# Two more raw tiles in the ring that loads the first FFN's weights and the conditioning matrix

## The chip, the cores and the metric

The kernel runs on one core of one Trainium2 chip. The metric is the device time of one execution in microseconds. The core has five engines with an instruction stream each: PE (matrix products), DVE (element-wise work), ACT (casts and activations), POOL, and SP, which here issues nearly all DMAs. Each works through its own stream in order and waits on semaphores of the others.

## The reference, cut to what matters

One layer of a diffusion backbone: 512 latent tokens and 256 context tokens of width 1024. The first part is what the change touches. All shifts, scales and gates come from one matrix product of a vector with `w_ada` (1024 x 9216), and the first FFN (width 2816, SwiGLU) runs on both token sets:

```python
mod_x = (silu(c) @ w_ada + b_ada).reshape(bsz, 9, 1, d)
mod_c = (silu(c_ctx) @ w_ada + b_ada).reshape(9, 1, d)

def ffn_sublayer(h, m, i, w_up, w_down):
    shift, scale, gate = sub_mod(m, i)
    a, b = split(modulate(h, shift, scale) @ w_up, 2)
    y = (silu(a) * b) @ w_down
    return post_ln(ALPHA * h + 0.5 * gate * y, ln_g[i], ln_b[i])

x = ffn_sublayer(x, mod_x, 0, ffn1_w_in, ffn1_w_out)
ctx = ffn_sublayer(ctx, mod_c, 0, ffn1_w_in, ffn1_w_out)
```

Neighbourhood attention, a gated delta rule and a second FFN follow; the change doesn't edit them.

## The kernel before

Every weight matrix comes from HBM in tiles of 128 x 1024 float32 (512 KB). A tile is loaded by SP into a raw tile `wr`, cast by ACT to `wh` (line 135) and split by DVE into the remainder `wl = wr - wh` (line 137); three matmuls (`wh` with the high and the low part of the activations, `wl` with the high part) then make one product of nearly full precision. A tile of the conditioning matrix (`w_adaT`) is also loaded into a `wr`, but is read by DVE alone: line 279 multiplies it with the vector and sums along the row (its result tile is `adap`), once for the latent tokens, or twice where the context needs the section too.

In the first FFN all raw tiles come from one function, `raw1` (line 320), in turn: two buffers of the pool `w` and one of the pool `w1x`, so a ring of three. SP issues a load when the reader of the load three places earlier is done. The loads of `Stream.fill` (line 172, up and down weights; two weight tiles make one unit f of the FFN's width, a and b of the SwiGLU), of `modulate_k` (line 351), of `ada_gen` (line 300) and of the tokens (lines 435, 474) share it. The first three units' weights are an exception: `start_f` (line 400) loads them into tiles `ac`.

The stages, with their place in the profiled span:

- 0 to 61.5 us: for each of eight slices k of the width, two matrix tiles give the latent shift and scale (`modulate_k`), PE transposes the normalised tokens (line 358), ACT modulates and splits them into `uxh` and `uxl`, and the products of units 0 to 2 with that slice are made (lines 411 to 413, accumulators `acc`).
- 61.5 to 126.5: units 3 to 7 for the latent tokens (lines 190 to 192, `ps<-uxh`), while `modulate_k` makes the context's shift and scale.
- 126.5 to 221.8: units 0 to 7 for the context (`ps<-uch`), then units 8 to 10 for both, with four matrix tiles a unit from `ada_gen` (`ada_step(4)`).
- 221.8 to 312: the down product of units 0 to 10 (line 209), latent, then context.
- 312 to 504: the second up-phase, units 11 to 21 for both token sets, each with four matrix tiles.
- from 504: the down product of units 11 to 21 and the rest of the layer.

```python
def up_phase(hx, hc, fs):
    for f in fs:
        A, B = ws.get(), ws.get()
        hx.append(h_x())
        ffn_unit(tp, pp, A, B, uxh, uxl, NX, *hx[-1])
        hc.append(h_c())
        ffn_unit(tp, pp, A, B, uch, ucl, NCT, *hc[-1])
        ada_step(4)
```

The order of instructions on each engine isn't written by hand: a scheduler in the build sets it with a timeline of its own, in which free buffers count. The pool `t1` (`tp`, line 343) holds the temporaries of the first FFN (`fs`, `adap`, `crow`) and is closed at line 484.

Of the kernel before, what the change touches and what calls it, by code (L numbers as in the profile page):

```python
# [18 lines left out]
P = 128  # L19
D = 1024  # L20
# [38 lines left out]
def body(ctx, tc, I, out, dbg=None):  # L59
# [4 lines left out]
    def pool(name, side="left", space=None):  # L64
        kw = dict(name=name, bufs=1, reuse_waits="tile")
        if space is not None:
            kw["space"] = space
        else:
            kw["side"] = side
        g = tc.tile_pool(**kw)  # L70
        st = ExitStack()
        p = st.enter_context(g)
        return p, st.close
# [3 lines left out]
    def tl(p, shape, tag, bufs=1, dt=F32):  # L77
        uid[0] += 1
        return p.tile(list(shape), dt, name=f"{tag}_{uid[0]}", tag=tag, bufs=bufs)
# [214 lines left out]
    def ada_gen(tp, wp, crow):  # L294
        for sec in range(2, 9):
            which = [(0, colx)] + ([(1, colc)] if sec < 5 else [])
            sl = slice(sec * 8, sec * 8 + 8)
            for k in range(KT):
                raw = raw1()
                nc.sync.dma_start(raw[:], I["w_adaT"][sec * KT + k])  # L300
                for w, col in which:
                    dot_cols(tp, raw, crow[:, w], col, sec * 8 + k)
                if k < KT - 1:
                    yield
            for w, col in which:
                V.scalar_tensor_tensor(col[:, sl], col[:, sl], float(sec % 3 == 1), bcol[:, sl], op0=ALU.add, op1=ALU.add)
                if (w, sec) in gates:
                    to_row(tp, pp, col[:, sl], gates[(w, sec)])
            yield
# [5 lines left out]
    wp, close_wp = pool("w")  # L315
    WB = 2
    wx, close_wx = pool("w1x")
    raws = [0]

    def raw1():  # L320
        raws[0] += 1
        return tl(wx, [P, D], "wr") if raws[0] % 3 == 0 else tl(wp, [P, D], "wr", WB)

    ap_, close_ap = pool("acc1")
    hcp, close_hcp = pool("hc1")
# [15 lines left out]

    hxp, close_hxp = pool("hx1", "right")
    tp, close_tp = pool("t1")
    xn = {"x": [], "c": []}

    def modulate_k(pp, kind, k):

        w, col, uh, ul, n = (0, colx, uxh, uxl, NX) if kind == "x" else (1, colc, uch, ucl, NCT)
        for sec in range(2):
            raw = raw1()  # L350
            nc.sync.dma_start(raw[:], I["w_adaT"][sec * KT + k])
            dot_cols(tp, raw, crow[:, w], col, sec * 8 + k)
        for sec in range(2):
            c0 = sec * 8 + k
            V.scalar_tensor_tensor(col[:, c0:c0 + 1], col[:, c0:c0 + 1], float(sec), bcol[:, c0:c0 + 1], op0=ALU.add, op1=ALU.add)
        ps = tl(pp, [P, n], "ps", PSB[0])
        for t, x_t in enumerate(xn[kind]):
            T.transpose(ps[:, t * P:(t + 1) * P], x_t[:, k * P:(k + 1) * P], ident)
        u32 = tl(tp, [P, NX], "fs", 2)
        S.activation(u32[:, 0:n], ps[:], AF.Identity, bias=col[:, k:k + 1], scale=col[:, 8 + k:9 + k])  # L360
        split(u32[:, 0:n], uh[:, k], ul[:, k])
# [71 lines left out]
    for t in range(2):  # L433
        raw = raw1()
        nc.sync.dma_start(raw[:], tok_src("c", t))
        xn["c"].append(tl(ap_, [P, D], f"ac{t}"))
        ln_norm(tp, xn["c"][t][:], raw, act=True)
# [43 lines left out]
    hx, hc = up_phase([], [], range(HF, NF))  # L481
    for _ in ada:
        pass
    close_tp()
    close_up()

# [953 lines left out]
    tp, close_tp = pool("t2")  # L1440
# [247 lines left out]
```

## Time and profile before

| what | us |
|---|---|
| median of 3 runs (lowest, highest) | 1540.94 (1540.72, 1541.74) |
| time of the profiled execution | 1542.48 |
| its span | 1540.7 |

| stretch of the span, us | PE busy | DVE busy | DMA share | GB/s |
|---|---|---|---|---|
| 0 to 61.5 | 47.33 | 44.95 | 0.79 | 271 |
| 61.5 to 126.5 | 60.76 | 41.42 | 0.66 | 209 |
| 126.5 to 221.8 | 95.30 | 65.47 | 0.59 | 187 |
| 221.8 to 316 | 93.92 | 41.79 | 0.47 | 151 |
| 316 to 504 | 181.72 | 115.17 | 0.59 | 188 |
| 504 to 1540 | 986.67 | 740.07 | 0.40 | 129 |

Rows of the profile name an engine, a line of the kernel, the operation, the tiles as out<-in and, in brackets, how long the engine stood idle before it and what ended that. Matmuls are pipelined and their ends are modelled, so a PE without idle time isn't always at its full pace; the number of matmuls in a stretch tells more. SPq is the queue of SP: how its DMA issues follow each other.

### The profile page before, as it was taken

The numbers are of one execution on the slowest core, as the hardware profiler recorded it, in microseconds if no ns is written. First come the engines' busy times: TensorE is split into PE (matmuls) and PEld (weight loads), VectorE is DVE, ScalarE is ACT, GpSimd is POOL, SyncE is SP. The second block draws the span as 40 slices with busy tenths as digits, with TensorE's granted clock in tenths as the row PEclk, the third lists the DMA queues.
The fourth block names the chain that finished last, engine by engine and source line by source line (L and its number), as shares of the span: only waits on it lengthen the run. The fifth ranks groups of instructions, "written<-read, shape, count | busy, mean of one in ns | idle before, by whom it ended". The sixth has DMA issues, their size and how long they took to land.

```text
span 1540.7 us, 23656 instructions
## 1 busy us (share of the span) xinstructions
PE 1465.7 (95%) x9221; PEld 1257.3 (82%) x9221; DVE 1048.9 (68%) x1792; ACT 604.2 (39%) x1005; POOL 228.7 (15%) x224
## 2 busy tenths in 40 slices
PE   6999999999999999999997799999999999999997
PEld 4779988888788888898976687867778999998886
DVE  8566672577555487577758887566578699887426
ACT  5435321212211335645633443366525455344310
POOL 0000000000000021132300101167532023220001
PEclk9999999999999999999999899999999999999999
DMA  9666563556555623332377544173353233324422
GB/s 320 201 200 207 180 193 101 187 178 205 181 181 178 200 106 125 99 101 90 99 203 202 153 130 132 64 254 120 110 191 117 89 110 124 110 97 151 137 83 82
DMA packets 107586, 230.72 MB, mean 150 GB/s; under 512 B 34177, under 2 KB 47825, under 8 KB 107473
## 3 DMA queue, kind: packets, MB, share of 16 engines
q1 hardware_dynamic: 105312, 221.79, 45.2%
q10 hardware_dynamic: 1586, 5.32, 0.9%
q0 software_dynamic: 576, 2.10, 0.4%
q8 instruction: 72, 1.18, 0.3%
q14 instruction: 40, 0.33, 0.1%
HBM read 206.33 MB, written 22.85 MB: 149 GB/s over the span
## 4 chain that ended last, share of the span: by engine, by line
PE 62%; DMA 14%; DVE 13%; issue 5%; ACT 3%; POOL 2%; SPq 1%; DVEq 0%; ACTq 0%; POOLq 0%
PE ps L209 18%; DMA wr<-in_w_adaT_dram 8%; PE pm L190 5%; PE pm L192 5%; PE pm L191 5%; PE ps L192 4%; PE ps L190 4%; PE ps L191 4%; PE ps L1475 3%; PE ps L1476 3%; PE ps L1477 3%; DVE wl L137 3%; PE pc L854 3%; DVE adap L279 2%; DMA wr<-in_up_dram 1%
## 5 line engine op out<-in xcount | busy, mean ns | idle before, releaser
L137 DVE TENSOR_TENSOR wl<-wr,wh 128x1024 fp32r<-128x1024 f32 (+1 forms) x215 | 265.4, 1240 | 169.9 <-ACT wh L135 169.6
L135 ACT CAST wh<-wr 128x1024 fp32r<-128x1024 f32 (+1 forms) x215 | 217.5, 1017 | 340.5 <-PE ps L209 76.2
L279 DVE SCALAR_TENSOR_TENSOR adap<-wr,crow 128x1024 f32<-128x1024 f32 x112 | 137.0, 1223 | 93.8 <-DMA wr<-in_w_adaT_dram 92.3
L192 PE MATMUL ps<-uxh,wl 128*128 128x512 f32 (+1 forms) x496 | 181.5, 367 | 5.7 <-DVE wl L137 5.7
L190 PE MATMUL ps<-uxh,wh 128*128 128x512 f32 (+1 forms) x496 | 181.5, 369 | 4.8 <-ACT wh L135 4.7
L191 PE MATMUL ps<-uxl,wh 128*128 128x512 f32 (+1 forms) x496 | 180.6, 365 | 0.2 <-DVE uxl L137 0.2
L112 POOL TENSOR_TENSOR rs<-ve,mhalf 128x1 f32<-128x1 f32 (+2 forms) x46 | 49.9, 1088 | 762.3 <-DVE ve L108 752.6
L190 PE MATMUL pm<-uxh,wh 128*128 128x512 f32 x320 | 133.0, 416 | 4.3 <-ACT spill L606 2.3
L192 PE MATMUL pm<-uxh,wl 128*128 128x512 f32 x320 | 128.4, 401 | 0.4 <-DVE wl L137 0.4
L191 PE MATMUL pm<-uxl,wh 128*128 128x512 f32 x320 | 127.8, 399 | 0.0
L192 PEld LDWEIGHTS ps<-uxh,wl 128*128 128x128 f32 x496 | 94.4, 190 | 24.5 <-DVE wl L137 9.9
L190 PEld LDWEIGHTS ps<-uxh,wh 128*128 128x128 f32 x496 | 94.3, 191 | 21.4 <-ACT wh L135 7.3
L191 PEld LDWEIGHTS ps<-uxl,wh 128*128 128x128 f32 x496 | 94.7, 191 | 14.4 <-DVE uxl L137 0.4
L190 PE MATMUL ps<-uch,wh 128*128 128x256 f32 x352 | 98.6, 280 | 0.0
L192 PE MATMUL ps<-uch,wl 128*128 128x256 f32 x352 | 98.3, 279 | 0.0
L191 PE MATMUL ps<-ucl,wh 128*128 128x256 f32 x352 | 98.3, 279 | 0.0
L209 PE MATMUL ps<-wh,hx 128*128 128x512 f32 x352 | 94.8, 389 | 0.0
L209 PEld LDWEIGHTS ps<-wh,hx 128*128 128x128 f32 x352 | 65.9, 188 | 13.5
L190 PEld LDWEIGHTS pm<-uxh,wh 128*128 128x128 f32 x320 | 61.8, 193 | 16.3 <-ACT spill L606 2.7
L135 ACT CAST hx<-fs 128x512 fp32r<-128x512 f32 x22 | 13.7, 620 | 154.0 <-DVE fs L272 154.0
L192 PEld LDWEIGHTS pm<-uxh,wl 128*128 128x128 f32 x320 | 61.5, 192 | 14.8 <-DVE wl L137 1.5
L191 PEld LDWEIGHTS pm<-uxl,wh 128*128 128x128 f32 x320 | 61.7, 193 | 10.7
(411 smaller groups left out, 3485.4 us busy)
## 6 DMA issues: line engine op xcount, KB each, us to landing
wr<-in_w_adaT_dram SPq DMA_DIRECT2D x88, 512.0 KB, 4.0
wr<-in_up_dram SPq DMA_DIRECT2D x80, 512.0 KB, 3.6
wr<-in_dn_dram SPq DMA_DIRECT2D x58, 512.0 KB, 3.6
wr<-in_win_dram SPq DMA_DIRECT2D x52, 512.0 KB, 3.9
rb<-in_up_dram SPq DMA_DIRECT2D x18, 512.0 KB, 3.5
wr<-in_w_o_dram SPq DMA_DIRECT2D x8, 512.0 KB, 4.1
ac<-in_up_dram SPq DMA_DIRECT2D x6, 512.0 KB, 5.0
Dt<-gcd SPq DMA_DIRECT2D x12, 256.0 KB, 5.4
```

What stands on the lines that cost most here:

```text
L112: G.tensor_tensor(rs[:], ve[:], mhalf[:, 0:n], ALU.pow)
L135: S.copy(hi, src)
L137: V.tensor_tensor(lo, src, hi.bitcast(F32), ALU.subtract)
L190: T.matmul(ps, a, uh[:, k, :], start=(k == 0), stop=False)
L191: T.matmul(ps, a, ul[:, k, :], start=False, stop=False)
L192: T.matmul(ps, b, uh[:, k, :], start=False, stop=(k == nk - 1))
L209: T.matmul(banks[t][d][:, c0:c1], a[:, sl], b[:, d * 512 + c0:d * 512 + c1], start=first and j == 0, stop=last and j == 2)
L279: V.scalar_tensor_tensor(pr[:], raw[:], 1.0, crow, op0=ALU.mult, op1=ALU.mult, accum_out=col[:, c:c + 1])
L854: last[0] = T.matmul(*a, **k).ins
L1475: T.matmul(ps[:], a, uh[:, k], start=k == 0, stop=False)
L1476: T.matmul(ps[:], a, ul[:, k], start=False, stop=False)
L1477: T.matmul(ps[:], b, uh[:, k], start=False, stop=k == 3)
```

## The change

`raw1` takes a second pool into its turn while `more[0]` is set: of five raw tiles, two come from `w`, two from `t1` and one from `w1x`. `more[0]` is set when `t1` is opened, ahead of the first stage, and cleared when the last matrix tile has been taken, just ahead of closing `t1`. The loads behind that use the ring of three again.

```diff
-    raws = [0]
+    raws, more = [0], [None]
 
     def raw1():
         raws[0] += 1
-        return tl(wx, [P, D], "wr") if raws[0] % 3 == 0 else tl(wp, [P, D], "wr", WB)
+        k = raws[0] % (5 if more[0] else 3)
+        return tl(more[0], [P, D], "wr", 2) if k > 2 else tl(wx, [P, D], "wr") if k == 0 else tl(wp, [P, D], "wr", WB)
...
     tp, close_tp = pool("t1")
+    more[0] = tp
...
     for _ in ada:
         pass
+    more[0] = None
     close_tp()
```

The scheduler's order moves with it on every engine. On SP, in the first stage, before (`wr` from `in_w_adaT` are matrix tiles, `ac` from `in_up` the weights of units 0 to 2):

```order
L351 DMA wr_207<-in_w_adaT_dram 128x1024
L351 DMA wr_211<-in_w_adaT_dram 128x1024
L351 DMA wr_258<-in_w_adaT_dram 128x1024
L400 DMA ac_61_226<-in_up_dram 128x1024
L351 DMA wr_262<-in_w_adaT_dram 128x1024
L351 DMA wr_321<-in_w_adaT_dram 128x1024
L400 DMA ac_65_233<-in_up_dram 128x1024
L351 DMA wr_325<-in_w_adaT_dram 128x1024
L400 DMA ac_75_277<-in_up_dram 128x1024
L351 DMA wr_358<-in_w_adaT_dram 128x1024
L351 DMA wr_362<-in_w_adaT_dram 128x1024
L400 DMA ac_79_284<-in_up_dram 128x1024
```

And the same place now (two lines of the file lower, so line 353 is 351 and 402 is 400):

```order
L353 DMA wr_321<-in_w_adaT_dram 128x1024
L402 DMA ac_61_226<-in_up_dram 128x1024
L353 DMA wr_325<-in_w_adaT_dram 128x1024
L353 DMA wr_358<-in_w_adaT_dram 128x1024
L402 DMA ac_65_233<-in_up_dram 128x1024
L353 DMA wr_362<-in_w_adaT_dram 128x1024
L353 DMA wr_395<-in_w_adaT_dram 128x1024
L353 DMA wr_399<-in_w_adaT_dram 128x1024
L402 DMA ac_75_277<-in_up_dram 128x1024
L353 DMA wr_432<-in_w_adaT_dram 128x1024
L353 DMA wr_436<-in_w_adaT_dram 128x1024
L402 DMA ac_79_284<-in_up_dram 128x1024
```

The last four `ac` loads stand behind two, two, four and four more matrix tiles than before.

On PE, at the end of the same stage, before (line 358 transposes the tokens for k = 7, `acc` are the accumulators of the six products):

```order
L411 MATMUL acc_290<-uxh_87,hx_286 128x512
L412 MATMUL acc_290<-uxl_88,hx_286 128x512
L413 MATMUL acc_290<-uxh_87,hx_287 128x512
L358 MATMUL ps_479<-ident_64,ax_15_104 128x128
L358 MATMUL ps_479<-ident_64,ax_16_106 128x128
L358 MATMUL ps_479<-ident_64,ax_17_108 128x128
L358 MATMUL ps_479<-ident_64,ax_18_110 128x128
L411 MATMUL acc_193<-uxh_87,wh_189 128x512
L411 MATMUL acc_200<-uxh_87,wh_196 128x512
L411 MATMUL acc_232<-uxh_87,wh_228 128x512
```

And what stands ahead of the products of the last slices now (line 413 is 411, 414 is 412, 415 is 413):

```order
L414 MATMUL acc_283<-uxl_88,hx_279 128x512
L415 MATMUL acc_283<-uxh_87,hx_280 128x512
L413 MATMUL acc_290<-uxh_87,hx_286 128x512
L414 MATMUL acc_290<-uxl_88,hx_286 128x512
L415 MATMUL acc_290<-uxh_87,hx_287 128x512
L413 MATMUL acc_193<-uxh_87,wh_189 128x512
L414 MATMUL acc_193<-uxl_88,wh_189 128x512
L415 MATMUL acc_193<-uxh_87,wl_190 128x512
L413 MATMUL acc_200<-uxh_87,wh_196 128x512
L414 MATMUL acc_200<-uxl_88,wh_196 128x512
```

The transposes `ps_479` have moved well ahead, and the 36 products of the last two slices follow each other without one between them.

On SP, in the second up-phase, before (line 300 loads matrix tiles, line 172 weight tiles; `wr_3643` and `wr_3649` are the two of one unit, `wr_3783` and `wr_3789` of the next):

```order
L172 DMA wr_3643<-in_up_dram 128x1024
L172 DMA wr_3649<-in_up_dram 128x1024
L300 DMA wr_3767<-in_w_adaT_dram 128x1024
L300 DMA wr_3779<-in_w_adaT_dram 128x1024
L300 DMA wr_3771<-in_w_adaT_dram 128x1024
L300 DMA wr_3775<-in_w_adaT_dram 128x1024
L172 DMA wr_3783<-in_up_dram 128x1024
L172 DMA wr_3789<-in_up_dram 128x1024
```

And now:

```order
L172 DMA wr_3643<-in_up_dram 128x1024
L300 DMA wr_3767<-in_w_adaT_dram 128x1024
L300 DMA wr_3638<-in_w_adaT_dram 128x1024
L300 DMA wr_3771<-in_w_adaT_dram 128x1024
L172 DMA wr_3789<-in_up_dram 128x1024
L300 DMA wr_3775<-in_w_adaT_dram 128x1024
L300 DMA wr_3907<-in_w_adaT_dram 128x1024
L172 DMA wr_3649<-in_up_dram 128x1024
L300 DMA wr_3911<-in_w_adaT_dram 128x1024
L300 DMA wr_3779<-in_w_adaT_dram 128x1024
L172 DMA wr_3783<-in_up_dram 128x1024
```

The two tiles of a unit no longer follow each other. Of those that are loaded later than before, `wr_3649` stands five rows further back in SP's whole order, `wr_3783` three and `wr_3924`, of the unit after, six; `wr_3789` stands four rows further ahead. From the down product of units 11 to 21 on, the order is the same but for a few rows that change places on each engine.

## The prediction

> **What bounds the kernel now.** I read the page's first part, then the busy time of the engines by stretch, then what PE waits for, and last the chain of waits in the stretch that loses time. On the page:
>
> ```profile
> span 1540.7 us, 23656 instructions
> PE 1465.7 (95%) x9221; PEld 1257.3 (82%) x9221; DVE 1048.9 (68%) x1792; ACT 604.2 (39%) x1005; POOL 228.7 (15%) x224
> PE ps L209 18%; DMA wr<-in_w_adaT_dram 8%; PE pm L190 5%; PE pm L192 5%; PE pm L191 5%; PE ps L192 4%; PE ps L190 4%; PE ps L191 4%; PE ps L1475 3%; PE ps L1476 3%; PE ps L1477 3%; DVE wl L137 3%; PE pc L854 3%; DVE adap L279 2%; DMA wr<-in_up_dram 1%
> ```
>
> PE is the bound as a whole, so only its losses can be won back. But 8% of the chain that ended last is loads of the conditioning matrix into `wr`, the raw tile that the change multiplies. `wr` is cast and split (ACT L135, DVE L137) or multiplied and summed (DVE L279). The next table, busy time by stretch, shows where PE pays (columns: stretch, its length, PE, PEld, DVE, ACT, POOL busy with instruction counts, granted clock, DMA share, GB/s).
>
> ```profile
> 20.00:40.00 20.00, 20.00 (x87) 15.84 (x86) 18.96 (x37) 10.89 (x14) 0.00 (x0) 1.00 0.93 308
> 61.50:126.50 65.00, 60.76 (x257) 48.51 (x257) 41.42 (x78) 23.09 (x39) 0.00 (x0) 0.95 0.66 209
> 312.40:378.75 66.35, 66.35 (x385) 58.65 (x384) 51.84 (x85) 14.12 (x21) 0.00 (x0) 1.00 0.57 183
> 395.35:504.30 108.95, 102.67 (x579) 87.23 (x577) 56.03 (x88) 23.15 (x39) 0.00 (x0) 1.00 0.56 177
> ```
>
> 312.4 to 378.75 holds four units of the second up-phase (96 matmuls each): 66.35 / 4 = 16.59 us a unit, PE without a gap. 395.35 to 504.3 holds six of the same units in 108.95 us, 18.16 each. DMA is at 0.56 and DVE at 56 of 109 us there, so neither is full. What PE waits for, in 61.5 to 126.5 (the first two rows) and in 316 to 504 (the last two); us, times, longest:
>
> ```profile
> PE ps L190 <- ACT wh L135: 2.7, 1, 2.7
> PE ps L192 <- DVE wl L137: 1.4, 2, 0.7
> ...
> PE ps L192 <- DVE wl L137: 4.3, 6, 1.6
> PE ps L190 <- ACT wh L135: 2.0, 4, 1.0
> ```
>
> PE waits for split weights. Why these are late is in DVE's timeline and in the chain of waits of the same 18 us:
>
> ```profile
> 446.19 1.23 DVE L279 SCALAR_TENSOR_TENSOR adap<-wr,crow 128x1024 f32<-128x1024 f32 x1 [1.66 <-DMA wr<-in_w_adaT_dram]
> 447.46 1.23 DVE L279 SCALAR_TENSOR_TENSOR adap<-wr,crow 128x1024 f32<-128x1024 f32 x1
> 453.16 1.23 DVE L279 SCALAR_TENSOR_TENSOR adap<-wr,crow 128x1024 f32<-128x1024 f32 x1 [4.46 <-DMA wr<-in_w_adaT_dram]
> 456.62 1.23 DVE L137 TENSOR_TENSOR wl<-wr,wh 128x1024 fp32r<-128x1024 f32 x1 [0.25 <-ACT wh L135]
> ...
> 447.46 1.24 DVE adap L279 x2
> 448.72 4.34 DMA wr<-in_w_adaT_dram
> ...
> DVE adap L279 <- DMA wr<-in_w_adaT_dram: 62.3, 25, 5.3
> ...
> 444.56 3.22 SPq L172 DMA_DIRECT2D wr<-in_up_dram  x2
> 448.72 10.95 SPq L300 DMA_DIRECT2D wr<-in_w_adaT_dram  x4
> ```
>
> This is a loop. The dot at 447.46 frees its tile; only then, at 448.72, does SP issue the next load; it lands 4.34 us later; DVE stands 4.46 us for it, and the gate product (L272) and the splits of weights that landed earlier stand behind that dot, because DVE works in order. From 317 to 505 DVE stands 62.3 us for such loads. A raw tile is held for issue, landing and reading: 3 tiles at 18.16 / 6 = 3.03 us a load (a unit takes two weight tiles and four of the matrix) are 9.1 us each. Five tiles with the same holding time would allow a load every 1.82 us, while PE at full pace asks for one every 16.59 / 6 = 2.77 us. So with five the ring is no bound there.
>
> **The change part by part, and the sum.** No arithmetic, transfer or byte goes away: the 512 KB loads and their readers are the same. Two tiles are added to the rotation, the scheduler's order moves with them, and after the second up-phase the ring has three again.
>
> *Second up-phase.* Six units at the undisturbed pace take 6 x 16.59 = 99.5 us, so 108.95 - 99.5 = 9.4 us are the loss. I take 9.4 as won; the lower bound is zero (the rivals), the upper bound is this loss itself. Next late would be DVE: 56 of 99.5 us, no bound; then the DMA engines: 177 GB/s x 108.95 / 99.5 = 194, against 308 that the same engines moved from 20 to 40 us.
>
> *Units 3 to 7 of the first up-phase (61.5 to 126.5).* Here the matmuls wait in the same way, and the clock falls once:
>
> ```profile
> 106.75 0.79 PE L190 MATMUL ps<-uxh,wh 128*128 128x512 f32 x1 [2.75 <-ACT wh L135]
> ...
> 311.96 0.39 PE L209 MATMUL ps<-wh,hc 128*128 128x512 f32 x1
> ...
> 221.91 54.23 PE ps L209 x239
> ...
> 103.40:106.80 3.40, 0.65 (x4) 0.23 (x2) 2.54 (x7) 1.04 (x1) 0.00 (x0) 1.00 0.47 141
> 106.80:110.20 3.40, 3.35 (x7) 2.25 (x8) 1.59 (x3) 1.92 (x3) 0.00 (x0) 0.50 0.87 227
> 110.20:113.60 3.40, 3.40 (x16) 2.78 (x16) 3.40 (x6) 0.62 (x1) 0.00 (x0) 1.00 0.73 243
> ```
>
> Waits: 2.7 + 1.4 = 4.1 us. Idle time is counted from a matmul's shown end, 0.39 us behind its start, while undisturbed ones start every 54.23 / 239 = 0.227 us (the rows at 311.96 and 221.91): 0.16 more for each wait, 0.5 for three. Behind the 2.75 us wait the granted clock is 0.50 for 3.4 us: 7 matmuls instead of 16, 9 x 3.4 / 16 = 1.9 us. Together 6.5 us. The Trainium skill (TensorE: Matmul & The Clock Gate, "HAM oscillation — how this bites in real kernels") puts the rule abstractly as no PE-idle gap over about 3.4 us. By that rule a gap of 2.75 us would be followed by no drop and removing it would give back no clock: the sum would be 1.9 us smaller. The trace has the drop after 2.75 us and decides. Loads rise here to 209 x 65 / 58.5 = 232 GB/s, DVE to 41.4 of 58.5 us; both fit.
>
> *Start (to 61.5).* From 20 to 40 us DVE is busy 18.96 of 20 and DMA 0.93, so more tiles buy no pace. What moves is order: PE's one wait at the end of the stage,
>
> ```profile
> 55.25 0.98 PE L411 MATMUL acc<-uxh,wh 128*128 128x512 f32 x3 [1.52 <-ACT uxh L135]
> 59.60 1.98 PE L290 MATMUL ps<-crow,one_row 1*128 1x512 f32 x4
> 62.40:65.80 3.40, 3.40 (x10) 2.65 (x9) 2.63 (x5) 2.00 (x4) 0.00 (x0) 0.50 0.89 287
> 65.80:69.20 3.40, 3.40 (x17) 2.77 (x16) 3.07 (x7) 0.82 (x2) 0.00 (x0) 0.99 0.19 39
> ```
>
> loses its reason, since the transposes for k = 7 now stand well ahead of the products that need them. I take 1.5. The clock's fall at 62.4 (10 matmuls for 17, 7 x 0.2 = 1.4 us) follows this wait and the L290 products; it can stay or go, so 0.7. The other side: four loads of the first units' weights are issued behind more of the matrix (below). The last was issued at 27.95; four places at 20 us x 308 GB/s = 11.7 loads, 1.7 us each, make it 6.8 us later:
>
> ```profile
> 27.95 0.33 SPq L400 DMA_DIRECT2D ac<-in_up_dram  x1
> DMA to landing us min/median/max: 4.0/5.0/7.8
> L137 DVE TENSOR_TENSOR hx<-ac,hx x3: 1220/1226/1227, 26.7 to 34.0; 128x1024 fp32r<-128x1024 f32 x3
> ```
>
> Issued at 34.8 it lands by 39.8 and is split by 42.2 (DVE's last such split was at 34.0, 6 us after its issue). Its 24 matmuls, 5.5 us, can be done in the 17 us to 59.6. I price it at 0, and up to +6.8 at the far end.
>
> *Context's down product (from 280 to 316).* Its only wait is 0.2 us; the ring's rows there are one load per six matmuls. I take 0.3, bounds 0 and 1.
>
> *From 504 on.* Ring and tiles are as before; a few rows swap places because the scheduler starts from other times. No resource is added. I take 0, bounds -4 and +4 (the size of the longest wait for a load shown above, 4.46 us).
>
> Sum: 9.4 + 6.5 + 1.5 + 0.7 + 0.3 = 18.4 us. The profiled execution took 1542.5 us (span 1540.7); less 18.4 is 1524.1. The median of the runs is 1540.94, 1.5 less than that execution, which gives **1522.5 us**.
>
> **Rivals.** *In part (0.15).* DVE stays in order, and in the changed rows more dots than before can stand ahead of a split. If a third to a half of the waits only move to another unit, 6 to 9 us of the 18 remain lost: 1528.5 to 1532. For it: 25 waits of DVE on this load, the longest 5.3 us, show that one late load holds everything. Against: a load that finds a free tile is issued before its turn, not after it.
>
> *No change (0.04).* The transfers themselves could be the limit, so that more of them at once only land later: 1541. For it: loads issued close together land later (4.0 to 7.8 us at the start, 3.4 to 4.8 from 400 to 500).
>
> ```profile
> DMA to landing us min/median/max: 3.4/3.9/4.8
> ```
>
> Against: 308 GB/s against the 177 in use. That the tiles aren't used at all is excluded by the rows of the order.
>
> *Slower (0.05).* In the second up-phase the order of SP now lets a unit's second weight tile be loaded behind a tile of the next unit and four of the matrix: `wr_3649` goes five places back, `wr_3783` three, `wr_3924` six. SP works in order, so if the ring keeps its pace of 3.03 us a load, these come 15, 9 and 18 us later. In hand is some 7 us (the loads issued at 444.56 and about 3 us later land in 3.4 to 4.8 and are multiplied from 456.6 on). PE then waits 8 + 2 + 11 = 21 us: 1562. It decides at the pace p: two more tiles ahead put 2p more in hand, so five and six places cost 5p - 7 - 2p and 6p - 7 - 2p, 5.4 us together at p = 2.77 (three places cost nothing), while the 36 loads of the six units win 36 x (3.03 - p), 9.4. The two are equal at p = 2.86; above it the new order loses more than the tiles win. Against it: at 3.03 a load each of five tiles would be held for 15 us, and the rows show 9.
>
> **How the numbers follow.** Forecast (0.76): 1522.5, own range 1517 to 1528 (downward 0.7 for the rest of the clock's fall, 0.7 in the down product and 4 behind 504; upward 0.7, 0.3 and 4). In part 0.15, no change 0.04, slower 0.05. The range 1517 to 1532 holds the forecast's own range, the late landing at the start (1529.3) and the case in part. A measurement of this kernel tells about 0.2% (3 us) from no change: faster 0.91 (forecast and part), same 0.04, slower 0.05.
>
> **What would show it.** Right: the last six units of the second up-phase in 99 to 101 us; PE's waits for `wl` and `wh` at L190 and L192 under 2 us in both stretches; no half clock between 100 and 125; DVE's 62.3 us for matrix loads far smaller, SP issuing them while three older ones are unread; DMA near 194 GB/s in the last six units. Wrong in the start: L411 to L413 waiting for `hx` weights between 30 and 45. Wrong in the order: PE waiting once in two units, several us at a time, for the second weight tile. If everything before 504 is 18 us earlier and the end is not, the rest lies behind.

## The result, and the profile after

The changed kernel takes 1528.59 us (median of 4 runs, 1525.19 to 1530.66), the kernel before 1541.34 us beside it (4 runs, 1540.72 to 1547.03). The ratio is 0.9904, its 95% interval 0.9887 to 0.992: faster by some 15 us. The profiled execution of the changed kernel is its slowest run, 1530.66 us. Three more series of it, shown below, have medians of 1525.76 to 1526.46; one execution in them, of 2926.64 us, stands apart from all others and is left out.

From the page of the changed kernel: its span, the first row of busy time, and the chain that ended last by line.

```profile
span 1528.8 us, 23646 instructions
PE 1462.6 (96%) x9221; PEld 1258.7 (82%) x9221; DVE 1050.0 (69%) x1792; ACT 605.4 (40%) x1005; POOL 226.8 (15%) x224
PE ps L209 19%; PE ps L190 8%; PE ps L192 8%; PE ps L191 8%; PE pm L190 5%; PE pm L192 5%; PE pm L191 5%; PE pc L857 2%; PE ps L1478 2%; PE ps L1480 2%; PE ps L1479 2%; DVE wl L137 2%; PE po L1266 1%; DMA T<-rd 1%; PE pt L1255 1%
```

Busy times are those of before, to 3 us on PE and 1 us on DVE: nothing was computed less. The matrix loads, 8% of the chain before, are no longer among the lines of the chain, and the products at L190 to L192 stand in their place.

Busy time by stretch of the changed kernel, at the places of the four rows quoted in the prediction (20 to 40 us; units 3 to 7; the first four units of the second up-phase; its last six):

```profile
20.00:40.00 20.00, 20.00 (x89) 15.63 (x89) 19.97 (x39) 10.88 (x14) 0.00 (x0) 1.00 0.98 365
59.30:118.60 59.30, 57.06 (x257) 46.47 (x257) 41.82 (x78) 23.77 (x40) 0.00 (x0) 1.00 0.69 231
303.60:369.95 66.35, 66.35 (x386) 58.76 (x385) 58.26 (x96) 15.54 (x24) 0.00 (x0) 1.00 0.71 231
386.55:486.00 99.45, 99.45 (x580) 88.00 (x578) 52.86 (x81) 23.75 (x37) 0.00 (x0) 1.00 0.50 165
```

The last six units take 99.45 us in place of 108.95 and PE has no gap; units 3 to 7 take 59.3 in place of 65, at full clock. In the first four units DMA now moves 231 GB/s in place of 183 and DVE handles 96 instructions in place of 85: the matrix is read ahead there, and the last six units have less of it left, 165 GB/s in place of 177. What is left of the waits for split weights, PE's from 59 to 119 (first row), and DVE's from 308 to 486 (the other two; before it had 62.3 us on the first of them):

```profile
PE ps L192 <- DVE wl L137: 2.2, 2, 1.9
...
DVE adap L279 <- DMA wr<-in_w_adaT_dram: 23.3, 19, 3.0
DVE fs L272 <- PE ps L192: 20.3, 12, 6.7
```

From 307 to 486 PE waits for nothing. DVE now waits for PE's products as long as for loads: the roles of the loop have turned round.

The end of the first stage in PE's timeline, where it had waited 1.52 us at 55.25:

```profile
57.05 0.39 PE L415 MATMUL acc<-uxh,hx 128*128 128x512 f32 x1
57.37 1.98 PE L290 MATMUL ps<-crow,one_row 1*128 1x512 f32 x4
59.28 0.50 PE L190 MATMUL ps<-uxh,wh 128*128 128x512 f32 x1
```

No wait, and units 3 to 7 begin at 59.3 in place of 61.5. The table sets the stages of both profiled executions side by side; each is read from the start of its first product to that of the next stage's. (Attention begins with the first `pm` product, takes in the delta rule and ends where the transposes that open the second FFN begin; these, 0.8 us, are in no row of the table.)

| stage, us | before | after | difference | predicted |
|---|---|---|---|---|
| start | 61.5 | 59.3 | -2.2 | -2.2 |
| units 3 to 7 | 65.1 | 59.3 | -5.8 | -6.5 |
| context's units, units 8 to 10, latent down product | 155.1 | 155.1 | 0 | 0 |
| context's down product | 30.8 | 29.9 | -0.9 | -0.3 |
| second up-phase | 191.9 | 182.4 | -9.5 | -9.4 |
| **to its end** | **504.3** | **486.0** | **-18.3** | **-18.4** |
| second down product and what follows it | 124.6 | 124.6 | 0 | 0 |
| attention | 533.6 | 535.9 | +2.3 | 0 |
| second FFN to the end | 377.4 | 381.5 | +4.1 | 0 |

Ahead of the second down product all that was predicted is there; 6.4 us of it are missing at the end. The rows of the last two stages, before and after (attention; the second FFN with its 0.8 us of transposes):

```profile
628.90:1162.60 533.70, 498.00 (x3668) 413.99 (x3669) 381.76 (x772) 249.74 (x474) 153.03 (x150) 0.98 0.45 138
1162.60:1540.70 378.10, 365.67 (x2423) 334.66 (x2421) 273.31 (x389) 149.37 (x225) 58.05 (x42) 0.99 0.33 111
```

```profile
610.60:1146.50 535.90, 501.15 (x3668) 415.95 (x3668) 380.85 (x770) 249.58 (x474) 153.24 (x149) 0.97 0.44 137
1146.50:1528.80 382.30, 367.52 (x2422) 335.54 (x2422) 275.11 (x389) 147.97 (x225) 55.52 (x42) 0.99 0.33 109
```

The instructions are the same to one or two. Either these stages differ from one execution to the next (in attention the granted clock is 0.97 against 0.98), or the changed order of rows costs something there. The experiments are about this, and about how many tiles the loop needs and where.

### The profile page after: what moved, and what is told of

The parts are those of the page before. It is cut to its first block, busy times and chain, and to the rows that moved or that the text cites. A ratio compares the mean times of both kernels' runs of the same rounds, so it can differ in the third digit from the quotient of the medians.

```text
span 1528.8 us, 23646 instructions
## 1 busy us (share of the span) xinstructions
PE 1462.6 (96%) x9221; PEld 1258.7 (82%) x9221; DVE 1050.0 (69%) x1792; ACT 605.4 (40%) x1005; POOL 226.8 (15%) x224
## 4 chain that ended last, share of the span: by engine, by line
PE 76%; DVE 10%; DMA 7%; issue 3%; ACT 2%; POOL 2%; SPq 0%; DVEq 0%; ACTq 0%; POOLq 0%
PE ps L209 19%; PE ps L190 8%; PE ps L192 8%; PE ps L191 8%; PE pm L190 5%; PE pm L192 5%; PE pm L191 5%; PE pc L857 2%; PE ps L1478 2%; PE ps L1480 2%; PE ps L1479 2%; DVE wl L137 2%; PE po L1266 1%; DMA T<-rd 1%; PE pt L1255 1%
## 5 line engine op out<-in xcount | busy, mean ns | idle before, releaser
L192 PE MATMUL ps<-uxh,wl 128*128 128x512 f32 (+1 forms) x496 | 179.6, 363 | 2.2 <-DVE wl L137 2.2
L190 PE MATMUL ps<-uxh,wh 128*128 128x512 f32 (+1 forms) x496 | 179.6, 365 | 0.0
L190 PE MATMUL pm<-uxh,wh 128*128 128x512 f32 x320 | 133.0, 416 | 4.1 <-ACT spill L609 2.1
L192 PE MATMUL pm<-uxh,wl 128*128 128x512 f32 x320 | 128.2, 401 | 0.7 <-DVE wl L137 0.7
L192 PEld LDWEIGHTS ps<-uxh,wl 128*128 128x128 f32 x496 | 93.7, 189 | 17.9 <-DVE wl L137 3.3
L190 PEld LDWEIGHTS ps<-uxh,wh 128*128 128x128 f32 x496 | 93.4, 189 | 14.3 <-issue 0.8
L190 PE MATMUL ps<-uch,wh 128*128 128x256 f32 x352 | 98.6, 280 | 0.0
L192 PE MATMUL ps<-uch,wl 128*128 128x256 f32 x352 | 98.3, 279 | 0.0
L190 PEld LDWEIGHTS pm<-uxh,wh 128*128 128x128 f32 x320 | 61.6, 193 | 16.3 <-ACT spill L609 3.0
L192 PEld LDWEIGHTS pm<-uxh,wl 128*128 128x128 f32 x320 | 61.7, 193 | 14.8 <-DVE wl L137 1.5
L190 PEld LDWEIGHTS ps<-uch,wh 128*128 128x128 f32 x352 | 66.1, 188 | 0.6
```

The lines of the kernel that those rows point to most:

```text
L190: T.matmul(ps, a, uh[:, k, :], start=(k == 0), stop=False)
L192: T.matmul(ps, b, uh[:, k, :], start=False, stop=(k == nk - 1))
```

## The experiments

A unit has six loads, so the 11 units of the second up-phase have 66, and stage time / 66 x number of tiles is how often a place of the ring comes round.

**The changed kernel again.** No edit.

> The changed kernel once more, to see what of its 528 us behind the second up-phase repeats. Theory A (the order of the rows behind 504 us of the kernel before costs it there): attention and its surroundings (from the first pm product to the second FFN's first transpose) 535 to 537 us again, the second FFN to the end 380.5 to 382, against 533.6 and 377.4 before; the front part (to the second down product) 486 +- 1. Rival B (chance: the granted clock fell in other places in that one execution): the two lengths differ from those by over 2 us and may be those of before; front 486 as well.

Median 1526.21 us (1523.7 to 1529.12, 4 runs), ratio 0.9888 [0.9869, 0.9906]. In the profiled execution the second up-phase ends at 486.9 us, attention takes 533.4 (533.6 before), the second FFN 381.7 (377.4 before). Theory A holds for the second FFN and fails for attention, whose excess was of that one execution.

**One more tile, not two.**

```diff
-        k = raws[0] % (5 if more[0] else 3)
-        return tl(more[0], [P, D], "wr", 2) if k > 2 else tl(wx, [P, D], "wr") if k == 0 else tl(wp, [P, D], "wr", WB)
+        k = raws[0] % (4 if more[0] else 3)
+        return tl(more[0], [P, D], "wr") if k > 2 else tl(wx, [P, D], "wr") if k == 0 else tl(wp, [P, D], "wr", WB)
```

> A ring of four instead of five (one more tile, not two). Behind the first FFN the rows stand as in the kernel before on every engine. Theory A: attention 533.6 +- 1 and second FFN to the end 377.4 +- 0.7, as before. Rival B: these lengths vary as they do in the changed kernel, or are longer as there because the work starts earlier. Front: a part of the 18.3 us; a load every 2.77 us needs tiles held for no more than 11.1 us, and they are held for 9.1, so the second up-phase should be within 3 us of its undisturbed length (182 to 186 us, 191.9 before), units 3 to 7 between 59 and 64. Time between 1525 and 1533.

Median 1535.03 us (1533.32 to 1541.55, 6 runs), ratio 0.995 [0.9931, 0.9968]. Start 61.2, units 3 to 7 64.4, second up-phase 185.5. From its profile: busy time in the last six units of the second up-phase (99.45 us with five tiles), then what PE and DVE wait for in the whole of it.

```profile
393.55:496.00 102.45, 100.28 (x578) 87.71 (x577) 54.77 (x86) 24.48 (x40) 0.00 (x0) 1.00 0.55 176
```

```profile
PE ps L192 <- DVE wl L137: 2.2, 3, 0.9
...
DVE adap L279 <- DMA wr<-in_w_adaT_dram: 60.5, 26, 4.6
```

The second up-phase is in its expected band, but units 3 to 7 (59 to 64 expected) and the time (1525 to 1533) are not. Theory A holds for the second FFN (377.1) and fails for attention, which takes 536.2 us with all its rows as before; that the lengths vary by themselves (B) stays possible.

By the prediction's loop (a tile is always held 9.1 us) four tiles would have been enough: a load every 2.3 us, where PE asks for one every 2.77. They are not: the stage is 3.1 us longer than with five. A place of the ring came round every 191.9 / 66 x 3 = 8.7 us with three tiles, 185.5 / 66 x 4 = 11.2 with four and 182.4 / 66 x 5 = 13.8 with five. That is a quotient, in which a place can also stand free. Matching each load issued in the stage with its readers in the traces gives the holding itself, from SP's issue to the end of the last reader: 8.5, 10.9 and 12.7 us on the mean. It also shows the loop directly: 66 of 68 loads before, 65 of 67 with four tiles and 64 of 66 with five are issued within 0.3 us of their place becoming free. The longer holding is that of the weight tiles (loads of `in_up`: 9.8, 17.1 and 19.3 us); tiles of the matrix are held for 7.8, 7.4 and 9.0. So weights that are loaded earlier wait longer for their readers, the holding time isn't a constant, and dividing it by the number of tiles promises too much.

DVE's wait for these loads hardly fell (62.3 to 60.5 us), though two thirds of PE's loss went (191.9 to 185.5, of 9.5): the idle time of an engine with slack doesn't measure what the loads cost.

**Four tiles for the first 16 loads, then five.** The tiles and everything else are as in the change; only the turn differs.

```diff
-        k = raws[0] % (5 if more[0] else 3)
+        n = 3 if not more[0] else 4 if raws[0] <= 16 else 5
+        k = (raws[0] - 1) % n + 1
+        k = 0 if k == 3 else 3 if k == 4 else 4 if k == 5 else k
```

> A ring of four for the first 16 loads, of five behind them. The rows of attention stand as in the changed kernel, those of the second FFN as in the kernel before. Theory A: front as in the changed kernel (486 +- 1.5), attention 535 to 537, second FFN to the end 377.4 +- 0.7: time about 4 us below the changed kernel. Rival B: second FFN to the end as in the changed kernel (381) or anything between; no difference of time beyond the interval.

Median 1524.96 us (1523.31 to 1530.34, 5 runs), ratio 0.9889 [0.9869, 0.9908]. Units 3 to 7 take 61.2 us, the second up-phase 182.4 and ends at 487.6; behind it the rows of attention stand as in the changed kernel, those of the second FFN as before the change. Theory A fails here: the second FFN takes 380.6 us with its old rows, attention 534.8, and the median is 1.25 us below that of the changed kernel, not 4. This kernel is the second means by which the order is tried (below).

**Five tiles up to unit 7 only.** `more[0]` is cleared where the context's shift and scale are done.

```diff
+    more[0] = None
     gates = {k: tl(dp, [8, P], "gate")[:] for k in ((0, 2), (1, 2), (0, 5), (0, 8))}
```

> The ring of five until the last of units 3 to 7 only, of three behind it; the rows behind the first FFN stand as in the changed kernel. All theories: start and units 3 to 7 as in the changed kernel (59.3 and 59.3 us), second up-phase 190 to 192 us as before. Theory A: attention 535 to 537, second FFN to the end 380.5 to 382, so the gain of the front (8 us) is mostly given back: time 1537 to 1540. Rival B: the two lengths as before, time 1531 to 1534.

Median 1535.48 us (1534.82 to 1536.64, 5 runs), ratio 0.9948 [0.9931, 0.9964]. Busy time in units 3 to 7 and in the last six units of the second up-phase, and PE's waits in the latter:

```profile
59.30:118.00 58.70, 58.45 (x258) 47.81 (x258) 41.76 (x78) 23.84 (x40) 0.00 (x0) 0.97 0.64 215
385.95:496.10 110.15, 103.55 (x580) 88.58 (x578) 56.73 (x89) 23.43 (x39) 0.00 (x0) 0.98 0.56 176
```

```profile
PE ps L192 <- DVE wl L137: 4.5, 5, 2.4
PE ps L190 <- ACT wh L135: 2.1, 3, 0.8
```

The early stages have their whole gain, the late one has none (110.15 us against 108.95 before; the second up-phase takes 193.1). The end of the second up-phase is at 496.1 us, 8.2 earlier than before, and the median 7.8 below the 1543.24 of before in this series: half the change gives nearly half the gain. Attention takes 533.4 us and the second FFN 379.8, and the time lies between the two bands, so neither theory holds in full.

**The kernel before, again**, for how much it varies by itself.

> The kernel before once more, for a second profile of its 1036 us behind the second up-phase. Order theory (the place-changes of rows behind 504 us cost some 4 us in the second FFN): second FFN to the end 377 to 378 again. Chance theory (that length moves by some microseconds between executions of the same program): it differs from 377.4 by over 1 us. Both: front (to the second down product) 504 +- 1, attention 533 to 537, ratio 1.

Median 1542.91 us (1538.47 to 1546.55, 12 runs); 1.001 [0.9996, 1.0024] against itself. Its profiled execution: attention 530.6, second FFN 376.2 us (533.6 and 377.4 in the first one). By what was expected this is the chance theory's outcome: the second FFN differs from 377.4 by 1.2 us, and the front (505.8) and attention leave their bands too. Attention varies by 3 us with nothing changed, units 3 to 7 (66.3 us here, 65.1 in the first profile) by 1.2.

**Five tiles from the second up-phase on.** The other half of the experiment before the last.

```diff
-    more[0] = tp
...
+    more[0] = tp
     hx, hc = up_phase([], [], range(HF, NF))
```

> Five tiles in the second up-phase alone, three ahead of it. Ring theory (the prediction's): start and units 3 to 7 as before (61.5 and 65), second up-phase 182.4 as in the changed kernel, so 9.5 of the front's 18 us: front 494 to 495, time 1531 to 1534. Rival (the second up-phase profits from the reserve that the earlier stages built up with five tiles): it stays over 184 us.

Median 1537.48 us (1532.29 to 1543.8, 12 runs), ratio 0.9983 [0.9966, 0.9999]. Busy time in its second up-phase:

```profile
309.70:492.10 182.40, 182.40 (x1058) 161.41 (x1058) 116.95 (x184) 44.15 (x67) 0.00 (x0) 1.00 0.57 185
```

PE stands nowhere, and the stage takes 182.4 us, although the ring came to it with no reserve from the stages ahead. So this gain comes from tiles in its own stage.

The early stages are less clear: the start takes 60.0 and units 3 to 7 take 63.2 us (61.5 and 65.1 before, 61.1 and 66.3 in its second profile), with three tiles as before but with other rows in the scheduler's order. So of the 8 us that five tiles win there, some 3 came in this one profile without them, and what the order or chance gives there was not tried apart from the tiles.

The whole gains less than the front, and less than the expected 1531 to 1534: the front ends 12.2 us earlier than before, and the median is 4.1 below the 1541.57 of before in this series (2.6 by the ratio). The profiled execution, at 1543.8 the slowest of the 12, has an attention stage of 541.9 us. Its extra time is at two places; busy time there, and rows of PE at the second:

```profile
1015.00:1021.80 6.80, 6.52 (x36) 5.00 (x38) 5.24 (x8) 4.93 (x15) 6.80 (x6) 0.53 1.05 381
1045.00:1055.20 10.20, 9.38 (x60) 7.23 (x59) 3.90 (x7) 4.83 (x14) 3.71 (x4) 0.52 0.11 32
```

```profile
1044.81 0.67 PE L1224 MATMUL pt<-ident,vst 128*128 128x128 f32 x4 [2.24 <-ACT pT L1257]
1046.30 1.12 PE L1266 MATMUL po<-pT,vw 128*64 128x128 f32 x8 [0.82 <-DVE vw L1225]
```

PE ran 17 us at about half clock, which is worth some 8 us. In all, attention has 47.7 us at half clock here, 20.4 to 30.8 in the other eleven profiles. In this kernel the rows of attention stand in a third order. Whether the order makes these falls is not shown: at the second place PE waits 0.79 and 1.64 us in the changed kernel run again and keeps full clock, but in the changed kernel's first profile it waits 0.79 and 1.88 us there and the clock falls as well:

```profile
1034.00:1040.80 6.80, 5.92 (x36) 4.65 (x36) 2.72 (x5) 4.16 (x13) 5.68 (x5) 0.51 0.21 69
```

Nor does one profile, of the slowest execution, explain why the median of the 12 lacks 8 of the 12.2 us. The second FFN takes 382.3 us here, as long as in the changed kernel, without the late load that is found there below.

**Four then five, and the changed kernel, twice more each.** The changed kernel and four-then-five have the same five tiles from the 17th load on and the same order in attention; in the second FFN rows on all five engines differ, from 78 to 135 us behind its start, and those of four-then-five stand as before the change. So the pair tries that order alone, but for the front.

> Four, then five raw tiles, once more (rows of the second FFN as before). Order theory: second FFN to the end nearer to 377.4 than to 381.5 this time, and the time lower than that of the changed kernel by 2 to 4 us in the same call. Chance theory: between 377 and 382 without a rule, the two times equal within 2 us. Front 487.6 +- 1.5.

> The changed kernel a third time, beside the one with four, then five. Order theory: second FFN to the end 381 to 382 a third time. Chance theory: it leaves that band. Front 486 to 487, units 3 to 7 59.0 to 59.3.

> The rule with four tiles at first once more, on the same chip as the changed kernel, for the term behind the first FFN. Theory 'order': the rows of the second FFN stand here as before the change, so PE loses nothing 160 to 180 us after that FFN's start (below 0.7 us), the stage takes 376 to 379 us and the median is 1.0 to 2.0 us below that of the changed kernel, although the front is some 0.5 us longer. Theory 'chance': the excess of the second FFN in the profiled executions came from where the granted clock fell; the loss in that stretch is as in the changed kernel and the median is equal to it or up to 0.5 us above.

> The changed kernel once more beside the run above. Theory 'order': PE loses 1 to 3 us 160 to 180 us after the start of the second FFN again, the stage takes 379 to 382 us, median 1525.5 to 1527. Theory 'chance': the loss there is below 1 us in this execution, or the median is no higher than that of the run above.

| run | median, us (runs) | ratio | second up-phase ends | attention | second FFN |
|---|---|---|---|---|---|
| four then five, first | 1524.96 (5) | 0.9889 | 487.6 | 534.8 | 380.6 |
| four then five, second | 1524.59 (4) | 0.99 | 486.3 | 532.4 | 378.8 |
| four then five, third | 1525.46 (6) | 0.9883 | 487.7 | 534.4 | 378.0 |
| changed, the result's | 1528.59 (4) | 0.9904 | 486.0 | 535.9 | 381.5 |
| changed, first again | 1526.21 (4) | 0.9888 | 486.9 | 533.4 | 381.7 |
| changed, second again | 1525.76 (5) | 0.9911 | 485.7 | 534.0 | 378.9 |
| changed, third again | 1526.46 (5) | 0.9893 | 485.2 | 533.8 | 381.5 |

By what was expected, the first pair (second of four-then-five, second again of the changed kernel) comes out as chance in two of three points: the second FFN of the changed kernel leaves its band (378.9), and the times are equal within 2 us; the second FFN of four-then-five is nearer to 377.4, as the order theory said. The last pair comes out as order: 378.0 and 381.5 us, medians 1.0 us apart, and PE waits 1.4 us in the stretch named in advance in the changed kernel and nowhere there in the other. In three series on one chip each the median of four-then-five is 1.0 to 1.25 us lower; by the ratios it is 0.2 us behind, 1.7 and 1.5 ahead. With 4 to 6 runs that spread over 2 to 7 us, and intervals that overlap, the times alone decide nothing.

The traces show a place, where PE's products stand still, 160 to 180 us behind the start of the second FFN. SP's load of the raw tile `rb`, the first product on `wh` behind it, what DVE waits for, and the first product of the next stretch are these before the change (L1475 is the product there, L1452 reads `rb`):

```profile
1330.69 0.33 SPq L1448 DMA_DIRECT2D rb<-in_up_dram  x1
...
1333.06 0.28 PE L1475 MATMUL ps<-uxh,wh 128*128 128x256 f32 x1
...
1334.13 0.69 DVE L1452 TENSOR_TENSOR s<-rb 128x512 f32<-128x512 f32 x1 [2.33 <-DMA rb<-in_up_dram]
...
1342.58 0.39 PE L190 MATMUL ps<-uxh,wh 128*128 128x512 f32 x1
```

The same four in the changed kernel (three lines of the file lower), and PE's waits there:

```profile
1317.66 0.33 SPq L1451 DMA_DIRECT2D rb<-in_up_dram  x1
...
1317.60 0.28 PE L1478 MATMUL ps<-uxh,wh 128*128 128x256 f32 x1
...
1321.59 0.69 DVE L1455 TENSOR_TENSOR s<-rb 128x512 f32<-128x512 f32 x1 [2.82 <-DMA rb<-in_up_dram]
...
1329.34 0.39 PE L190 MATMUL ps<-uxh,wh 128*128 128x512 f32 x1
```

```profile
PE ps L1478 <- DVE sn L1499: 0.8, 1, 0.8
PE ps L1478 <- DVE sn L1500: 0.3, 1, 0.3
```

And three of them in the third run of four-then-five (two lines lower again):

```profile
1311.98 0.33 SPq L1453 DMA_DIRECT2D rb<-in_up_dram  x1
...
1315.98 0.28 PE L1480 MATMUL ps<-uxh,wh 128*128 128x256 f32 x1
...
1325.88 0.39 PE L190 MATMUL ps<-uxh,wh 128*128 128x512 f32 x1
```

Before, SP issues the load of `rb` 2.4 us ahead of that product, in four-then-five 4.0 us ahead, and the stretch to the next products takes 9.5 and 9.9 us. In the changed kernel the load is issued when the product starts; DVE's sum that reads it begins 4.0 us behind that product, against 1.1 before, with the sums of products (`sn`) queued behind it; PE waits for these, and the same stretch takes 11.7 us.

Over all profiled executions: with the second FFN's rows as before (before twice, four tiles, four-then-five three times) the load leads by 1.2 to 4.0 us and the stretch takes 9.5 to 10.1, 9.87 on the mean; in the four of the changed kernel it leads by -0.7 to 0.1 and the stretch takes 11.6 to 12.8, 12.02 on the mean. That is 2.15 us on the mean, and the two groups don't overlap. Five tiles from the second up-phase on, with a third order of these rows, has a lead of 2.7 us and a stretch of 9.9. The kernel with five tiles to unit 7 has the changed rows too, but the load leads by 1.1 us there and the stretch takes 10.3: what costs is the late load, not the rows at the place itself, which are alike in both; that the exchanged rows, 35 to 90 us earlier, make DVE late is likely, and which of them wasn't tried.

In the whole time four-then-five doesn't keep the 2.15 us: its front ends 1.3 us later on the mean, and PE goes through the 300 products up to this place in 35.3 us in its three profiles, against 34.0 in all of before and of the changed kernel (last section).

The second FFN takes 376.2 to 377.4 us in the three profiles with all rows as before, 378.0 to 380.6 in four-then-five and 378.9 to 381.7 in the changed kernel, so beside the 2.15 us some 2 us on the mean are left. Part of them lies 37 to 43 us behind its start, ahead of the first exchanged row: PE waits there for ACT's `y`, 1.2 to 2.9 us in the twelve profiles, and in seven of them the granted clock is 0.50 for 3.4 us behind the wait. In the changed kernel's first profile:

```profile
1186.41 1.09 PE L146 MATMUL ps<-ident,y 128*128 128x128 f32 x8 [2.14 <-ACT y L128]
...
1187.70:1191.10 3.40, 3.40 (x19) 3.40 (x18) 0.69 (x2) 3.11 (x9) 0.00 (x0) 0.50 0.86 286
```

Nineteen matmuls instead of the 30 of the next 3.4 us are a loss of some 1.2 us. It comes in all four profiles of the changed kernel, in one of three of four-then-five and in one of three with all rows as before. Why so often in the changed kernel stays open; the order of rows in the second FFN can't be the reason.

## Why the prediction was right, and where it was off

- **Second up-phase (-9.4):** right, in size and place: -9.5 in the profile, and 182.4 us in every profiled execution with five tiles in that stage, against 191.9 to 193.1 with three. The reason was right in its loop (a load is issued when a tile comes free) and too simple in its number: holding time grows with the ring, from 8.5 to 12.7 us. That five are enough was luck of the margin, 1.82 us a load by the prediction against 2.77, and 12.7 / 5 = 2.5 by the holding measured; the same reasoning gave 2.28 for four, and that failed.
- **Units 3 to 7 (-6.5):** -5.8 in the profiled execution, -6.0 to -6.6 in the three others; the half clock at 106.8 is gone, as predicted. The nearness is partly luck. A wait of 1.91 us for `wl` ahead of 96 us came in place of the 2.75 us one (the two waits left make 2.2 us, where under 2 was the sign), and the half clock at 62.4, which the prediction counted under the start, lies behind 61.5 and so in this stage: 6.5, less some 2.5 for the two waits left, and 1.4 for that fall come to 5.4.
- **Start (-2.2):** -2.2. The wait of 1.52 us went as the transposes had moved; the other 0.7 us of the prediction were for the clock, which fell only behind this stage, so that the sizes agree is luck and where the remaining half microsecond was won is open. The fall of the clock is away in the profiled execution and there again at 60 to 61 us in two of the other three, so half its price was a fair stake. The start varies too: 59.3 to 60.5 us in the four profiles of the changed kernel. The feared late landing of the first units' weights did not come: PE waits for no `hx` weights there, and 20 to 40 us ran at 365 GB/s in place of 308, which the prediction had not expected either.
- **Context's down product (-0.3):** -0.9, inside its bounds.
- **From 504 on (0, bounds -4 and +4):** this is the term that was off. The profiled execution has +6.4, of which +2.3 in attention is that execution's own (533.4 to 534.0 in the other three, 530.6 to 536.2 with the rows as before). About +2.15 comes each time: one late load in the second FFN, 800 us behind the change, where no tile or loop was edited and only rows had changed places. The other 1.9 us of the second FFN in that profile are open; the half clock 41 us into it is not among them, as the first profile of before has it too. The prediction allowed for all this by its bounds and took the middle: that a few exchanged rows cost nothing was an assumption, and the sign could not be read from the order.
- **The sum:** by ratios the kernel gains 13.7 to 17.3 us (1 - ratio times some 1542), not 18.4. With the 2.15 us the steps make 16.2. The predicted 1522.5 is 3.3 to 4 us under the three later medians and 6.1 under the first.
- **The rivals:** the time falls on the edge of "in part" (1528.5 to 1532), but its mechanism isn't there, since PE waits for nothing in the second up-phase and the loss isn't in another unit. "Slower" would show as waits of several us for `wl`; none is there. DMA in the last six units was to be near 194 GB/s and is 165, since the matrix runs ahead into the units before.

## What to carry to other kernels

A ring of raw tiles that are held for landing and for a busy reader should be sized by trying one more, not by dividing a measured holding time, because tiles that come earlier wait longer (8.5, 10.9 and 12.7 us here with three, four and five); stage times with three, four and five tiles were 191.9, 185.5 and 182.4 us here, and 182.4 is the time without a wait. Read the gain from the waits of the engine that bounds, not from the idle time of the one that reads the tiles. Where a scheduler sets the order, a change in one stage can cost a few us in a stage far behind it, so compare the stages one by one between several executions, and try a second variant that differs in that order alone. Expect that it differs in something else as well, and go by the place in the trace, not by the two medians.

## What the hardware showed that was not expected

The granted clock doesn't fall behind every short wait, and where it falls differs between executions of one kernel. In the changed kernel PE was busy 1.52 of the 3.4 us ahead of 96.0, with the 1.91 us wait among them, and kept full clock; before, 0.65 of 3.4 busy with the 2.75 us wait was followed by half clock:

```profile
92.60:96.00 3.40, 1.52 (x9) 0.96 (x7) 2.99 (x6) 0.62 (x1) 0.00 (x0) 1.00 0.31 99
96.00:99.40 3.40, 3.37 (x15) 2.80 (x16) 3.40 (x9) 1.74 (x3) 0.00 (x0) 1.00 0.82 253
```

Elsewhere a wait of 1.93 us (37 to 43 us into the second FFN, changed kernel, second again) was followed by half clock, and waits of 1.96 and 1.98 us at the same place in two other profiles were not. Such falls lie at other places from one execution of a kernel to the next: the two profiles of the kernel before have 24.0 and 20.4 us at half clock in attention, which differs by 3 us between them, and the changed kernel has 24.0 to 30.8. Each is worth as much as a term of the prediction.

PE's pace without a wait isn't one number either. The same 300 products, some 135 to 170 us into the second FFN, take 34.0 us in each of the six profiles of before and of the changed kernel, and 35.3 in each of the six of the other kernels, at full granted clock in both. Twenty us of them in the changed kernel and in the third run of four-then-five:

```profile
1290.00:1310.00 20.00, 20.00 (x178) 20.00 (x178) 18.42 (x27) 8.59 (x14) 6.45 (x4) 1.00 0.31 104
1287.00:1307.00 20.00, 20.00 (x172) 20.00 (x171) 18.40 (x27) 8.97 (x14) 6.06 (x4) 1.00 0.30 95
```

A product starts every 113 ns in one and every 118 ns in the other. The cause is open; PE shows as busy throughout in both.
